# Expert-choice MoE inside a three-layer kernel: one-hot gather and scatter in exact high and low parts, 15 weight slots, weights in 8 KB runs

## Chip, cores and metric

One NeuronCore of a Trainium2 chip runs the whole program in one launch. The metric is device microseconds (us) of that launch. All matrices are float32 in memory; the program may use fp32r (the single-pass float32 form of TensorE) where the values allow it.

## The reference

The program is one block with an expert-choice mixture of experts, followed by two layers of another block. Only the experts of the first block are touched (S = 512 tokens, D = 1024, 16 experts, each takes its 64 best tokens):

```python
def expert_choice_ffn(h, router_w, w_gate, w_up, w_down):
    cap = CAPACITY_FACTOR * T // N_EXPERTS            # 64
    aff = jax.nn.softmax(jnp.einsum('btd,de->bte', h, router_w), axis=-1)
    gate, idx = lax.top_k(jnp.swapaxes(aff, 1, 2), cap)
    xin = jax.vmap(lambda hb, ib: hb[ib])(h, idx)
    hid = jax.nn.silu(jnp.einsum('becd,edf->becf', xin, w_gate)) * jnp.einsum('becd,edf->becf', xin, w_up)
    y = jnp.einsum('becf,efd->becd', hid, w_down) * gate[..., None]
    return scatter_add(y, idx)
...
h2 = modulate(layer_norm(x), sh2, sc2)
x = layer_norm_affine(ALPHA * x + gt2 * expert_choice_ffn(h2, ...), ln2_g, ln2_b)
```

## The kernel before

The tokens stand in NT = 4 tiles `K.x[i]` of 128 tokens by 1024 channels. `first_out` ends the mixer and calls `moe_token` for each token tile: `normed` (L752) writes the normalised tokens `m.h[i]`, PE transposes them (L834), ACT copies them out (L835) and a router product gives the 16 affinities `m.aff`. In `moe`, top-k on VectorE (DVE) turns them into ranks `m.pos`.

The loop over experts goes by pairs (e0, e0 + 1). DVE compares the ranks with a row of numbers: the one-hot matrix P (L895), [token, expert of the pair x slot]. **Gather**: for each of KD = 8 channel blocks, PE multiplies the block of `m.h[i]` by P and sums over the four token tiles (L902); the modulation is applied on the way out of PSUM, on DVE or ACT by turns (L905, L907), which gives XT, [channel, slot]. PE transposes P (L911), ACT copies it to PT (L912), and PE takes each slot's gate value by a product of P with the affinities (L918). **Gate and up**: 64 slots by 1024 outputs in two 64-column tiles of PE, L929. Silu is on ACT (L934), the product with up and the gate value on DVE (L935); PE transposes it (L938), ACT copies it (L946, hidT). **Down** is L952. DVE multiplies by the modulation into Y (L957). **Scatter**: PT times Y, for four token tiles by two halves of 512 channels (L959), and DVE adds the result to x (L967, L969). The last pair scatters into PSUM banks that already hold x (L944, L975) and goes straight to the next LayerNorm (L740, L983).

A product of two float32 operands is one instruction in the program and two records in the trace; fp32r is one record.

Each expert's weights come in twelve loads of 1 MiB, [128, 2, 1024], issued by SP through `K.raw` (L78). The slots are three rings: two of five slots (`K.use_ring(c, 5, 5)`, open from the mixer's end) and `ring2` with eight, opened in `moe`; `turns` says which ring the next load takes. An issue waits on SP's queue until its slot's matmuls are done, and holds what is queued behind it.

PE's order is not the order of the program text: a list scheduler places instructions by readiness and priority, so gathers of the next pair and scatters of the last stand between gate and up matmuls. PSUM has banks for gu (2), tr (2, gather), rt (1), py (1) and sc (2, scatter).

Of the kernel before, what the change touches and what calls it, by code (L numbers as in the profile page):

```python
# [8 lines left out]
F32 = mybir.dt.float32  # L9
# [742 lines left out]

def normed(K, out, x, spread):

    nc = K.nc
    m, r = ln_stats(K, halves(x))
    if spread:
        nc.scalar.activation(out, x, AF.Identity, scale=r, bias=ln_bias(K, m, r))
    else:
        nc.vector.tensor_scalar(out, x, m, r, op0=OP.subtract, op1=OP.mult)  # L760
# [18 lines left out]


def moe_start(K, c):

    nc = K.nc
    m = Moe()
    m.keep = K.pool(c, "e_keep", 1, side="right")
    K.use_ring(c, 5, 5, side="right")
    hp = K.pool(c, "e_h", 1, side="right")
    m.h = [hp.tile([128, D], F32, name=f"h{i}") for i in range(NT)]
    m.aff = m.keep.tile([128, NT, NE], F32, name="aff")
    m.pos = m.keep.tile([128, NT, NE], F32, name="pos")  # L790
    m.cols = m.keep.tile([128, 16], F32, name="ecols")
    m.iota = m.keep.tile([128, CAP], F32, name="iota")
    nc.gpsimd.iota(m.iota, pattern=[[1, CAP]], base=1, channel_multiplier=0, allow_small_or_imprecise_dtypes=True)
    return m


def moe_router(K, m, pool, router_w, mods):
# [7 lines left out]
    m.bias = pool.tile([128, NE], F32, name="bias")  # L805
    rw = pool.tile([128, KD, 128], F32, name="nT")[:, :, :NE]
    nc.sync.dma_start(rw, dram(router_w, 0, [[NE, 128], [128 * NE, KD], [1, NE]]))
    rows = pool.tile([128, 128], F32, name="lt")[:16]
    nc.sync.dma_start(rows, dram(mods, 1024, [[128, 16], [1, 128]]))
    ones = pool.tile([128, 128], F32, name="lt")  # L810
    nc.gpsimd.memset(ones, 1.0)
    p = K.ps("ex")
    nc.tensor.transpose(p[:, :16], rows, K.ident[:16, :16])
    cols = m.cols
    nc.vector.tensor_copy(cols, p[:, :16])
    nc.vector.scalar_tensor_tensor(m.rw[:, :, :NE], rw, -1.0, cols[:, 8:, None].to_broadcast([128, KD, NE]), op0=OP.mult, op1=OP.mult)
# [7 lines left out]
def moe_token(K, m, pool, i):  # L824

    nc = K.nc
    n = m.h[i]
    normed(K, n, K.x[i], i < NT - 1)
    nT = pool.tile([128, KD, 128], F32, name="nT")
    for g in range(2):  # L830
        p = K.ps()
        for j in range(4):
            k = g * 4 + j
            nc.tensor.transpose(p[:, j * 128:(j + 1) * 128], n[:, k * 128:(k + 1) * 128], K.ident)  # L834
        nc.scalar.copy(nT[:, g * 4:g * 4 + 4].rearrange("p a b -> p (a b)"), p)  # L835

    p = K.ps()
# [15 lines left out]
def moe(K, m, wg, wu, wd, mods):  # L853

    nc, tc = K.nc, K.tc
    with ExitStack() as c:
        K.use_banks(c, gu=2, tr=2, rt=1, py=1, sc=2)
        xp = K.pool(c, "e_x", KD)
        gp = K.pool(c, "e_p", 2)

        K.rings.append(K.pool(c, "ring2", 8))
        yp = K.pool(c, "e_y", 1)
        gt2 = K.bcast(yp, mods[3], "gt2")
        turns = itertools.cycle([0, 1] * 5 + [2] * 8)
        with ExitStack() as c2:
# [23 lines left out]
        for e0 in range(0, NE, 2):  # L889

            XT = [xp.tile([128, 2 * CAP], F32, name="XT") for _ in range(KD)]
            P = gp.tile([128, NT, 2, CAP], F32, name="P")
            Pm = P.rearrange("p i e c -> p i (e c)")
            for i in range(NT):
                nc.vector.tensor_tensor(P[:, i], m.iota[:, None, :].to_broadcast([128, 2, CAP]),  # L895
                                        m.pos[:, i, e0:e0 + 2, None].to_broadcast([128, 2, CAP]), op=OP.is_equal)
            for k in range(KD):
                if k % 4 == 0:
                    p4 = K.ps("tr")
                p = p4[:, k % 4 * 128:(k % 4 + 1) * 128]  # L900
                for i in range(NT):
                    nc.tensor.matmul(p, m.h[i][:, k * 128:(k + 1) * 128], Pm[:, i], start=i == 0, stop=i == NT - 1)  # L902
                sh, sc = m.cols[:, k:k + 1], m.cols[:, 8 + k:9 + k]
                if k % 2:
                    nc.scalar.activation(XT[k], p, AF.Identity, scale=sc, bias=sh)  # L905
                else:
                    nc.vector.tensor_scalar(XT[k], p, sc, sh, op0=OP.mult, op1=OP.add)  # L907
            PT = yp.tile([128, S], F32, name="PT")
            pp = K.ps("rt")
            for i in range(NT):  # L910
                nc.tensor.transpose(pp[:, i * 128:(i + 1) * 128], Pm[:, i], K.ident)  # L911
            nc.scalar.copy(PT, pp)  # L912
            y = yp.tile([128, D], F32, name="Y")
            for e in (e0, e0 + 1):
                p = K.ps("rt")
                for i in range(NT):
                    for h in range(2):
                        nc.tensor.matmul(p[h * 64:(h + 1) * 64, 0:1], P[:, i, e - e0], m.aff[:, i, e:e + 1],  # L918
                                         start=i == 0, stop=i == NT - 1, tile_position=(0, h * 64))
# [3 lines left out]
                for w in (wg, wu):  # L923
                    p = K.ps("gu")
                    for k0 in range(0, KD, 2):
                        r = K.raw([128, 2, D], dram(w, (e * D + k0 * 128) * D, [[D, 128], [128 * D, 2], [1, D]]), next(turns))
                        for k in range(k0, k0 + 2):
                            for h in range(2):
                                nc.tensor.matmul(p[h * 64:(h + 1) * 64], XT[k][:, (e - e0) * CAP:(e - e0 + 1) * CAP],  # L929
                                                 r[:, k - k0, h * 512:(h + 1) * 512], start=k == 0, stop=k == KD - 1,  # L930
                                                 tile_position=(0, h * 64))
# [16 lines left out]
                for f0 in range(0, KD, 2):  # L948
                    r = K.raw([128, 2, D], dram(wd, (e * D + f0 * 128) * D, [[D, 128], [128 * D, 2], [1, D]]), next(turns))
                    for f in range(f0, f0 + 2):  # L950
# [907 lines left out]
def first_out(K, F, I, cm, mods):  # L1858

    nc = K.nc  # L1860
    with ExitStack() as c:
# [35 lines left out]
        scan_finish(K, F, 2)  # L1897
        scan_finish(K, F, 3)
        moe_router(K, m, tp, I["router_w"], mods)
        acc.append([K.ps("ex") for _ in range(2)])  # L1900
# [91 lines left out]
```

## Time and profile before

| what | value |
|---|---|
| runs | median 3489.3 us of 3 (3488.88 to 3494.43) |
| profiled execution | 3489.0 us, its span 3487.2 us |
| mean granted clock of TensorE | 0.95 |
| busy over the span | PE 90%, DVE 61%, ACT 39%, POOL (GpSimd) 30% |
| token phase | 760 to 813 us: PE 29.5 us busy, DVE 43.8, ACT 9.8, POOL 8.3 of 53 |
| experts | 813 to 1345 us: PE 519.4 us busy, DVE 99.5, ACT 40.0 of 532; clock 0.98; DMA share 0.92 |
| two layers after them | from 1345 us on |

All times of rows are microseconds from the span's start. A time behind a group of matmuls is from its first start to its modelled end, which overlaps the next; the step from one start to the next is what one costs. `PEclk` is the clock that the throttle granted, 1.00 being 2.4 GHz and 0.50 being 1.2 GHz. The DMA share is the mean busy share of 16 DMA engines; it can read slightly above 1.

### The profile page before, as it was taken

The numbers are of one execution on the slowest core, as the hardware profiler recorded it, in microseconds if no ns is written. First come the engines' busy times: TensorE is split into PE (matmuls) and PEld (weight loads), VectorE is DVE, ScalarE is ACT, GpSimd is POOL, SyncE is SP. The second block draws the span as 40 slices with busy tenths as digits, with TensorE's granted clock in tenths as the row PEclk, the third lists the DMA queues.
The fourth block names the chain that finished last, engine by engine and source line by source line (L and its number), as shares of the span: only waits on it lengthen the run. The fifth ranks groups of instructions, "written<-read, shape, count | busy, mean of one in ns | idle before, by whom it ended". The sixth has DMA issues, their size and how long they took to land. (4 is left out here: it accounts for less than half of the span.)

```text
span 3487.2 us, 52482 instructions
## 1 busy us (share of the span) xinstructions
PE 3130.2 (90%) x20683; PEld 2450.0 (70%) x20683; DVE 2141.1 (61%) x3732; ACT 1356.0 (39%) x2630; POOL 1063.5 (30%) x1071
## 2 busy tenths in 40 slices
PE   6989876777999997999999989998999989989998
PEld 4765455653434334998877678987898977779987
DVE  5667984463211116765767666757856776858657
ACT  3446564221000003443456543434433455634433
POOL 3134473040000004342431243424432341233423
PEclk9999987988999998999999999999999999999999
DMA  5335265548999992322332123222322322213222
GB/s 208 112 118 192 99 200 169 198 151 323 400 387 373 376 352 79 111 84 98 104 96 66 39 71 109 85 97 95 100 97 97 98 79 64 67 49 111 84 99 95
DMA packets 284775, 508.53 MB, mean 146 GB/s; under 512 B 30430, under 2 KB 206384, under 8 KB 279408
## 3 DMA queue, kind: packets, MB, share of 16 engines
q1 hardware_dynamic: 267520, 487.35, 39.7%
q10 hardware_dynamic: 16336, 17.13, 1.5%
q8 instruction: 162, 2.65, 0.3%
q0 software_dynamic: 672, 0.70, 0.1%
q14 instruction: 85, 0.70, 0.1%
HBM read 473.66 MB, written 31.47 MB: 145 GB/s over the span
## 5 line engine op out<-in xcount | busy, mean ns | idle before, releaser
L100 DVE TENSOR_TENSOR wl<-raw,wh 128x1024 fp32r<-128x1024 f32 (+2 forms) x346 | 395.0, 1155 | 213.3 <-ACT wh L99 212.7
L105 PE MATMUL ps<-hTh,wh 128*128 128x256 f32 (+1 forms) x1656 | 493.4, 301 | 14.7 <-ACT hTh L238 12.5
L99 ACT CAST wh<-raw 128x1024 fp32r<-128x1024 f32 (+2 forms) x348 | 312.6, 920 | 458.0 <-PE ps L107 163.2
L106 PE MATMUL ps<-hTl,wh 128*128 128x256 f32 (+1 forms) x1656 | 489.2, 297 | 0.5 <-DVE hTl L239 0.5
L107 PE MATMUL ps<-hTh,wl 128*128 128x256 f32 (+1 forms) x1656 | 476.8, 297 | 3.4 <-DVE wl L100 3.3
L105 PEld LDWEIGHTS ps<-hTh,wh 128*128 128x128 f32 x1656 | 320.8, 195 | 27.9 <-ACT hTh L238 14.2
L297 POOL TENSOR_TENSOR tmp<-raw 128x512 f32<-128x512 f32 x176 | 246.4, 1407 | 292.0 <-DMA raw<-in_w_ffn_gate_dram 231.4
L106 PEld LDWEIGHTS ps<-hTl,wh 128*128 128x128 f32 x1656 | 321.2, 194 | 10.3 <-DVE hTl L239 1.7
L106 PE MATMUL ps<-wl,hh 128*128 128x512 f32 x832 | 324.0, 389 | 0.0
L107 PEld LDWEIGHTS ps<-hTh,wl 128*128 128x128 f32 x1656 | 314.5, 194 | 12.6 <-DVE wl L100 5.4
L107 PE MATMUL ps<-wh,hl 128*128 128x512 f32 x832 | 322.4, 389 | 0.0
L105 PE MATMUL ps<-wh,hh 128*128 128x512 f32 x832 | 303.6, 390 | 2.8 <-DVE hl L511 2.8
L115 POOL TENSOR_TENSOR rs_o<-rs_t,mhalf 128x1 f32<-128x1 f32 (+1 forms) x46 | 36.1, 811 | 848.7 <-DVE rs_t L114 847.7
L100 DVE TENSOR_TENSOR wl<-tmp,wh 128x1024 fp32r<-128x1024 f32 x176 | 244.6, 1390 | 56.9 <-ACT wh L99 55.8
L297 POOL TENSOR_TENSOR tmp<-raw,tmp 128x512 f32<-128x512 f32 x88 | 122.6, 1393 | 480.0 <-DVE wl L100 480.0
L929 PE MATMUL gu<-raw,XT 128*64 128x512 f32 x1024 | 250.7, 600 | 0.0
L99 ACT CAST wh<-tmp 128x1024 fp32r<-128x1024 f32 x176 | 184.4, 1048 | 92.8 <-POOL tmp L297 63.7
L105 PEld LDWEIGHTS ps<-wh,hh 128*128 128x128 f32 x832 | 155.5, 188 | 34.1 <-DVE hl L511 3.3
L107 PEld LDWEIGHTS ps<-wh,hl 128*128 128x128 f32 x832 | 156.2, 188 | 32.5
L106 PEld LDWEIGHTS ps<-wl,hh 128*128 128x128 f32 x832 | 156.3, 188 | 31.7
L929 PEld LDWEIGHTS gu<-raw,XT 128*64 128x64 f32 x1024 | 70.4, 136 | 133.7 <-issue 125.7
L294 DVE TENSOR_TENSOR u<-u,ps 128x256 f32<-128x256 f32 x308 | 127.6, 414 | 50.6 <-PE ps L107 27.2
(558 smaller groups left out, 7381.6 us busy)
## 6 DMA issues: line engine op xcount, KB each, us to landing
raw<-in_exp_w_gate_dram SPq DMA_DIRECT2D x64, 1024.0 KB
raw<-in_exp_w_up_dram SPq DMA_DIRECT2D x64, 1024.0 KB
raw<-in_exp_w_down_dram SPq DMA_DIRECT2D x64, 1024.0 KB
raw<-in_w_ffn_gate_dram SPq DMA_DIRECT2D x44, 1024.0 KB
raw<-in_w_ffn_up_dram SPq DMA_DIRECT2D x44, 1024.0 KB
raw<-in_w_ffn_down_dram SPq DMA_DIRECT2D x44, 1024.0 KB
raw<-in_w_ada_dram SPq DMA_DIRECT2D x24, 1024.0 KB
raw<-in_w_in_dram SPq DMA_DIRECT2D x36, 512.0 KB
```

Source lines behind the costliest of these rows:

```text
L99: nc.scalar.copy(h3, src)
L100: (engine or nc.vector).tensor_tensor(l3, src, h3.bitcast(F32), op=OP.subtract)
L105: mm(out, lhs[0], rhs[0], start=start, stop=False)
L106: mm(out, lhs[0], rhs[1], start=False, stop=False)
L107: mm(out, lhs[1], rhs[0], start=False, stop=stop)
L115: self.pow = nc.gpsimd.tensor_tensor(o[:, :n], t[:, :n], self.mhalf[:, :n], op=OP.pow)
L294: self.K.nc.vector.tensor_tensor(o, a, b, op=OP.add)
L297: self.K.nc.gpsimd.tensor_tensor(o, a, b, op=op)
L929: nc.tensor.matmul(p[h * 64:(h + 1) * 64], XT[k][:, (e - e0) * CAP:(e - e0 + 1) * CAP], r[:, k - k0, h * 512:(h + 1) * 512], start=k == 0, ...
```

## The change

Four things, all in the experts:

- **Gather.** Each normalised token is split into `hh` (the value as fp32r, an ACT copy) and `hl` (the rest, a POOL subtract), in halves of 512 channels (L856 and L857 of the changed file). P is written as fp32r, for four experts at once, so the gather runs once per two pairs with 256 columns and two fp32r products (`hh`, `hl`) per token tile. The gather's tiles take half a PSUM bank each.
- **Scatter.** Y is split likewise into Yh and Yl (DVE product, ACT copy, DVE subtract); PT is fp32r, and each scatter tile is two fp32r products.
- **Slots.** `ring2` has five slots instead of eight, 15 in all; `turns` follows.
- **Loads.** A load takes two neighbouring rows per partition, so that each partition reads 8 KB in one run. Channel 2p + r of a block of 256 then stands on partition p, and everything that meets the weights' rows follows that order: `normed` writes it, the router weights and modulation columns are loaded in it, and silu and the product are written through `pairs_apart` (the product in two halves of 256 columns).

```diff
+def pairs_apart(x):
+    n = x.shape[1] // 256
+    return x.rearrange("p (a r q) -> p a q r", a=n, r=2)
+def in_pairs(x):
+    return x.rearrange("p (a q r) -> p a q r", a=x.shape[1] // 256, r=2)
...
-def normed(K, out, x, spread):
+def normed(K, out, x, m, r, nm=None):
+    out, x = pairs_apart(out), in_pairs(x)
...
-    m.h = [hp.tile([128, D], F32, name=f"h{i}") for i in range(NT)]
+    m.hh, m.hl = ([hp.tile([128, D], F32R, name=f"{n}{i}") for i in range(NT)] for n in ("mh", "ml"))
...
+    for h, l, x in zip(halves(m.hh[i]), halves(m.hl[i]), n):
+        nc.scalar.copy(h, x)
+        nc.gpsimd.tensor_tensor(l, x, h.bitcast(F32), op=OP.subtract)
...
-        gp = K.pool(c, "e_p", 2)
-        K.rings.append(K.pool(c, "ring2", 8))
+        gp = K.pool(c, "e_p", 1)
+        K.rings.append(K.pool(c, "ring2", 5))
-        turns = itertools.cycle([0, 1] * 5 + [2] * 8)
+        turns = itertools.cycle([0, 1] * 5 + [2] * 5)
...
+            if e0 % 4 == 0:
+                XT = [xp.tile([128, 4 * CAP], F32, name="XT") for _ in range(KD)]
+                P = gp.tile([128, NT, 4, CAP], F32R, name="P")
...
-                    nc.tensor.matmul(p, m.h[i][:, k * 128:(k + 1) * 128], Pm[:, i], start=i == 0, stop=i == NT - 1)
+                    for i in range(NT):
+                        for n, h in enumerate((m.hh[i], m.hl[i])):
+                            nc.tensor.matmul(p, h[:, k * 128:(k + 1) * 128], Pm[:, i], start=i + n == 0, stop=i + n == NT)
...
-                        r = K.raw([128, 2, D], dram(w, (e * D + k0 * 128) * D, [[D, 128], [128 * D, 2], [1, D]]), next(turns))
+                        r = K.raw([128, 2, D], dram(w, (e * D + k0 * 128) * D, [[2 * D, 128], [D, 2], [1, D]]), next(turns))
...
-                nc.scalar.activation(sl, pg[0], AF.Silu)
-                nc.vector.scalar_tensor_tensor(sl, sl, gc, pg[1], op0=OP.mult, op1=OP.mult)
+                nc.scalar.activation(pairs_apart(sl), in_pairs(pg[0]), AF.Silu)
+                for a in range(2):
+                    q = slice(a * 256, a * 256 + 256)
+                    nc.vector.scalar_tensor_tensor(pairs_apart(sl[:, q]), pairs_apart(sl[:, q]), gc, in_pairs(pg[1][:, q]),
+                                                   op0=OP.mult, op1=OP.mult)
...
-                    nc.vector.tensor_tensor(y[ro, sl], py[h * 64:(h + 1) * 64], gt2[ro, sl], op=OP.mult)
+                    y = tp.tile([128, 512], F32, name="sil")[ro]
+                    nc.vector.tensor_tensor(y, py[h * 64:(h + 1) * 64], gt2[ro, sl], op=OP.mult)
+                    nc.scalar.copy(yh[ro, sl], y)
+                    nc.vector.tensor_tensor(yl[ro, sl], y, yh[ro, sl].bitcast(F32), op=OP.subtract)
...
-                nc.tensor.matmul(p, PT[:, i * 128:(i + 1) * 128], y[:, h * 512:(h + 1) * 512], start=start, stop=True)
+                for n, t in enumerate((yh, yl)):
+                    nc.tensor.matmul(p, PT[:, i * 128:(i + 1) * 128], t[:, h * 512:(h + 1) * 512], start=start and n == 0, stop=n == 1)
...
```

The scheduler's order changes with it. First PE around the transposes of silu (L938 before, L966 after; gu are gate and up, tr the gather, sc the scatter, py the down product), at an expert in the middle of the loop. Before:

```order
L929 MATMUL gu<-raw,XT 64x512 x4
L902 MATMUL tr<-P,h_7403 128x128
L902 MATMUL tr<-P,h_7404 128x128
L902 MATMUL tr<-P,h_7405 128x128
L902 MATMUL tr<-P,h_7406 128x128
L938 MATMUL rt<-ident,sil 128x128 x4
L902 MATMUL tr<-P,h_7403 128x128
L902 MATMUL tr<-P,h_7404 128x128
L902 MATMUL tr<-P,h_7405 128x128
L902 MATMUL tr<-P,h_7406 128x128
L952 MATMUL py<-raw,hidT 64x512 x12
```

And now, at two experts that follow one another:

```order
L943 MATMUL rt<-aff,P 64x1 x8
L954 MATMUL gu<-raw,XT 64x512 x12
L966 MATMUL rt<-ident,sil 128x128 x4
L980 MATMUL py<-raw,hidT 64x512 x4
L943 MATMUL rt<-aff,P 64x1 x8
L980 MATMUL py<-raw,hidT 64x512 x12
L954 MATMUL gu<-raw,XT 64x512 x32
L966 MATMUL rt<-ident,sil 128x128 x4
L980 MATMUL py<-raw,hidT 64x512 x4
```

Before, gather products stood on either side of the transposes; now gate and up, transposes and down follow one another with nothing between. Over the stage the runs of gather products between others go from 42 to 18, those of scatter products from 42 to 32.

Second, POOL in the token phase (rs_o is the reciprocal root of a LayerNorm; raw the weights of the mixer's last product). Before:

```order
L115 TENSOR_TENSOR rs_o<-rs_t,mhalf 128x8 x2
L1877 TENSOR_TENSOR raw<-raw 128x1024 x4
L811 MEMSET lt 128x128
L1877 TENSOR_TENSOR raw<-raw 128x1024 x4
L115 TENSOR_TENSOR rs_o<-rs_t,mhalf 128x1 x11
```

And now (L1910 is L1877 of before):

```order
L115 TENSOR_TENSOR rs_o<-rs_t,mhalf 128x8
L1910 TENSOR_TENSOR raw<-raw 128x1024 x4
L115 TENSOR_TENSOR rs_o<-rs_t,mhalf 128x8
L1910 TENSOR_TENSOR raw<-raw 128x1024 x4
L115 TENSOR_TENSOR rs_o<-rs_t,mhalf 128x1 x3
L857 TENSOR_TENSOR ml_7407<-fin,mh_7403 128x512 x2
L115 TENSOR_TENSOR rs_o<-rs_t,mhalf 128x1 x2
L857 TENSOR_TENSOR ml_7408<-fin,mh_7404 128x512 x2
L115 TENSOR_TENSOR rs_o<-rs_t,mhalf 128x1 x2
L857 TENSOR_TENSOR ml_7409<-fin,mh_7405 128x512
L115 TENSOR_TENSOR rs_o<-rs_t,mhalf 128x1
```

The subtracts for `hl` stand between the reciprocals of the token tiles, and one reciprocal of the mixer moved behind four multiplies of raw.

## Rows read from the trace of the kernel before

**Rows 1.** The page, busy time by engine.

```profile
PE 3130.2 (90%) x20683; PEld 2450.0 (70%) x20683; DVE 2141.1 (61%) x3732; ACT 1356.0 (39%) x2630; POOL 1063.5 (30%) x1071
```

**Rows 2.** Stretches: busy by engine (instructions), then PEclk, DMA share, GB/s.

```profile
813.00:1345.00 532.00, 519.35 (x2544) 213.07 (x2544) 99.45 (x198) 40.04 (x74) 1.05 (x2) 0.98 0.92 359
850.00:900.00 50.00, 50.00 (x242) 20.41 (x240) 10.22 (x20) 3.01 (x6) 0.00 (x0) 1.00 1.02 409
```

**Rows 3.** Waits of SP's queue, 813 to 1320: total us, times, longest.

```profile
SPq L78 <- PE gu L929: 295.2, 118, 18.4
SPq L78 <- PE py L952: 109.8, 51, 9.5
```

**Rows 4.** Timeline of SP's queue (start, us with waiting): first refill, last weight loads.

```profile
824.61 0.37 SPq L78 DMA_DIRECT2D raw<-in_exp_w_down_dram  x1
...
1285.31 11.71 SPq L78 DMA_DIRECT2D raw<-in_exp_w_down_dram  x4
```

**Rows 5.** Timeline of PE (start, us, records) at two places of the stage.

```profile
900.81 1.98 PE L959 MATMUL sc<-Y,PT 128*128 128x512 f32 x4
902.73 1.94 PE L929 MATMUL gu<-raw,XT 128*64 128x512 f32 x8
904.59 1.16 PE L902 MATMUL tr<-P,h 128*128 128x128 f32 x8
905.68 0.63 PE L918 MATMUL rt<-aff,P 128*64 128x1 f32 x16
...
1131.07 1.95 PE L902 MATMUL tr<-P,h 128*128 128x128 f32 x16
1132.86 0.60 PE L911 MATMUL rt<-ident,P 128*128 128x128 f32 x4
```

**Rows 6.** Timeline of PE outside it: fp32r products of 512 and 256 columns.

```profile
754.72 0.39 PE L107 MATMUL ps<-wh,fin 128*128 128x512 f32 x1
...
756.99 0.39 PE L105 MATMUL ps<-wh,fin 128*128 128x512 f32 x1
...
1399.78 0.28 PE L107 MATMUL ps<-T2h,wl 128*128 128x256 f32 x1
...
1402.78 0.28 PE L105 MATMUL ps<-T4h,wh 128*128 128x256 f32 x1
```

**Rows 7.** Waits of PE, 813 to 1337: total us, times, longest.

```profile
PE rt L938 <- DVE sil L935: 4.2, 4, 1.2
PE py L952 <- ACT hidT L946: 3.7, 5, 0.7
...
PE rt L918 <- ACT PT L912: 1.5, 2, 0.7
```

**Rows 8.** Groups by line, 813 to 1346: busy us, mean ns, idle before.

```profile
L969 DVE TENSOR_TENSOR x<-x,sc 128x512 f32<-128x512 f32 x48 | 33.0, 687 | 87.8 <-PE sc L959 87.8
...
L935 DVE SCALAR_TENSOR_TENSOR sil<-sil,gc,gu 128x512 f32<-128x512 f32 x16 | 11.9, 746 | 44.1 <-PE gu L929 28.7 <-issue 15.0
...
L946 ACT COPY hidT<-rt 128x512 f32<-128x512 f32 x16 | 9.4, 585 | 74.3 <-PE rt L938 74.3
```

**Rows 9.** Stretches behind three of PE's waits (columns as in rows 2).

```profile
1101.60:1108.40 6.80, 5.96 (x16) 2.18 (x18) 0.00 (x0) 0.58 (x1) 0.00 (x0) 0.50 0.08 20
...
1169.90:1176.70 6.80, 6.07 (x16) 2.00 (x18) 0.00 (x0) 0.58 (x1) 0.00 (x0) 0.50 0.19 69
1234.00:1242.00 8.00, 6.36 (x46) 2.52 (x44) 0.90 (x2) 0.59 (x1) 0.00 (x0) 1.00 1.00 376
```

**Rows 10.** Timeline of DVE at the stage's end.

```profile
1341.33 0.70 DVE L740 BATCH_NORM_STATS2 bn<-sc 128x6 f32<-128x512 f32 x1 [1.87 <-PE sc L959]
```

**Rows 11.** Timelines of POOL and of DVE at the mixer's end.

```profile
710.49 10.64 POOL L1877 TENSOR_TENSOR raw<-raw 128x1024 f32<-128x1024 f32 x4
...
713.30 2.84 DVE L1656 TENSOR_TENSOR x<-x,fin 128x512 f32<-128x512 f32 x1
```

**Rows 12.** A stretch with loads of the modulation weights (columns as in rows 2).

```profile
20.00:30.00 10.00, 5.71 (x30) 2.20 (x33) 8.66 (x17) 0.00 (x0) 4.57 (x7) 1.00 1.02 416
```

More of the change, by code (lines that the diff above doesn't have):

```diff
@@ L750, in ln_rows @@
     K.nc.vector.tensor_scalar(out, x, m, r, op0=OP.subtract, op1=OP.mult)
[L753 removed]
+def normed(K, out, x, m, r, nm=None):
     nc = K.nc
[L756 to L758 removed]
+    out, x = pairs_apart(out), in_pairs(x)
+    if nm is not None:
+        nc.scalar.activation(out, x, AF.Identity, scale=r, bias=nm)
     else:
@@ L805, in moe_router @@
     m.bias = pool.tile([128, NE], F32, name="bias")
[L806 to L809, printed above, removed]
+    nT = pool.tile([128, KD, 128], F32, name="nT")
+    rw = nT[:, 0].rearrange("p (a x) -> p a x", a=KD // 2)
+    nc.sync.dma_start(rw, dram(router_w, 0, [[2 * NE, 128], [256 * NE, KD // 2], [1, 2 * NE]]))
+    rows = nT[:8, 1:3].rearrange("p a b -> p (a b)")
+    rw = rw.rearrange("p a (r e) -> p (a r) e", r=2)
+    nc.sync.dma_start(rows, dram(mods, 1024, [[256, 8], [1, 256]]))
     ones = pool.tile([128, 128], F32, name="lt")
@@ L812, in moe_router @@
     p = K.ps("ex")
-    nc.tensor.transpose(p[:, :16], rows, K.ident[:16, :16])
+    for r in range(2):
+        nc.tensor.transpose(p[:, r * 8:r * 8 + 8], rows[:, r::2], K.ident[:8, :8])
     cols = m.cols
-    nc.vector.tensor_copy(cols, p[:, :16])
+    nc.vector.tensor_copy(cols.rearrange("p (v r) -> p v r", r=2), p[:, :16].rearrange("p (r v) -> p v r", r=2))
     nc.vector.scalar_tensor_tensor(m.rw[:, :, :NE], rw, -1.0, cols[:, 8:, None].to_broadcast([128, KD, NE]), op0=OP.mult, op1=OP.mult)
@@ L826, in moe_token @@
     nc = K.nc
-    n = m.h[i]
-    normed(K, n, K.x[i], i < NT - 1)
+    n = m.n
+    mean, r = ln_stats(K, halves(K.x[i]))
+    nm = ln_bias(K, mean, r) if i < NT - 1 else None
+    for o, x in zip(n, halves(K.x[i])):
+        normed(K, o, x, mean, r, nm)
     nT = pool.tile([128, KD, 128], F32, name="nT")
@@ L908, in moe @@
-            PT = yp.tile([128, S], F32, name="PT")
+            if e0 % 4 == 0:
+                XT = [xp.tile([128, 4 * CAP], F32, name="XT") for _ in range(KD)]
+                P = gp.tile([128, NT, 4, CAP], F32R, name="P")
+                Pm = P.rearrange("p i e c -> p i (e c)")
+                for i in range(NT):
+                    nc.vector.tensor_tensor(P[:, i], m.iota[:, None, :].to_broadcast([128, 4, CAP]),
+                                            m.pos[:, i, e0:e0 + 4, None].to_broadcast([128, 4, CAP]), op=OP.is_equal)
+                for k in range(KD):
+                    if k % 2 == 0:
+                        p4 = K.ps("tr")
+                    p = p4[:, k % 2 * 256:(k % 2 + 1) * 256]
+                    for i in range(NT):
+                        for n, h in enumerate((m.hh[i], m.hl[i])):
+                            nc.tensor.matmul(p, h[:, k * 128:(k + 1) * 128], Pm[:, i], start=i + n == 0, stop=i + n == NT)
+                    sh, sc = m.cols[:, k:k + 1], m.cols[:, 8 + k:9 + k]
+                    if k % 2:
+                        nc.scalar.activation(XT[k], p, AF.Identity, scale=sc, bias=sh)
+                    else:
+                        nc.vector.tensor_scalar(XT[k], p, sc, sh, op0=OP.mult, op1=OP.add)
@@ L948, in moe @@
                 for f0 in range(0, KD, 2):
-                    r = K.raw([128, 2, D], dram(wd, (e * D + f0 * 128) * D, [[D, 128], [128 * D, 2], [1, D]]), next(turns))
+                    r = K.raw([128, 2, D], dram(wd, (e * D + f0 * 128) * D, [[2 * D, 128], [D, 2], [1, D]]), next(turns))
                     for f in range(f0, f0 + 2):
@@ L1898, in first_out @@
         scan_finish(K, F, 3)
+        m.n = [F.fin.tile([128, 512], F32, name="fin") for _ in range(2)]
         moe_router(K, m, tp, I["router_w"], mods)
```

28 lines of the change are left out of this document (7 added, 21 removed).

## Prediction, before the changed kernel ran

> **What bounds the kernel now.** I first read the page's line of engines: TensorE (PE) is busy 90% of the span, no other engine above 61% [rows 1]. But the change touches one stage only, the experts, so I read that stage by itself, in the view of stretches: from 813 to 1345 us PE is busy 519 of 532 us, and in 850 to 900 all 50 of 50, while the DMA engines are at share 1.02 with 409 GB/s there and 0.92 over the stage [rows 2]. Both look full, so the question is which ends last. The waits of SP's queue, which issues the weight loads, answer it: it waits 295 us for gate and up matmuls (L929) and 110 us for down matmuls (L952) to free a slot [rows 3], and the four last are issued from 1285.3 over 11.71 us, so by 1297 us [rows 4], 48 us before the stage ends. DMA waits for PE; PE is the bound, DMA is close behind. So what the change takes off PE counts in full until the loads are reached.
>
> **Gather.** Before: 8 pairs x 8 channel blocks x 4 token tiles x 2 records, which is 512 records of 128x128. Sixteen in a row start 1.79 us before the next instruction, 0.112 us each [rows 5]. Where a run of eight stands between 64-column gate/up matmuls it takes 1.09 us instead of 0.90, so about 0.2 us per run goes into changing over. The order of before has 42 runs: 512 x 0.112 + 42 x 0.2 = 65.7 us. After: 4 groups x 8 blocks x 4 tiles x 2 (high, low) = 256 fp32r records of 128x256, in 18 runs. Such records start 0.12 us apart in the feed-forward stage: 25 steps in 3.00 us [rows 6]. So 256 x 0.12 + 18 x 0.2 = 34.3, **-31 us**. With no cost of changing over it would be -27.
>
> **Scatter.** 64 tiles of 128x512, each two records before. Four records next to gate/up take 1.92 us [rows 5], less 0.2 that is 0.43 each. After, a tile is two fp32r records (Yh, Yl), which start 0.227 us apart: 10 steps in 2.27 us [rows 6]. The last 8 tiles, at the stage's end, are paced by VectorE (below), so 56 tiles count: before 112 x 0.43 + 42 runs x 0.2 = 56.6; after 112 x 0.227 + 32 runs x 0.2 = 31.8. **-25 us** (-23 without the runs).
>
> **What shrinks comes out of the cover.** Each expert has a chain PE gate/up, ACT silu, DVE product, PE transposes, ACT copy, PE down product. PE hides it by other matmuls where the order has some to put there. It waited 4 times for the product (4.2 us, at most 1.2) and 5 times for the copy (3.7 us) [rows 7]; three of these are doubles, both waits of one expert, at 1101, 1169 and 1236. With half as many gather records and whole pairs without any, the scheduler's new order has 10 places where gate/up, transposes and down stand directly behind one another, 2 more with the second wait alone and 1 with the first. At 4.2/4 = 1.05 and 3.7/5 = 0.74 us, and 0.1 more since the product is now two halves of 256 columns (the 512 took 0.746 [rows 8], two halves lie between that and twice that): 11 x 1.15 + 12 x 0.74 = 21.5 against 7.9, **+14 us**. For a silu that writes with a stride there is no row; between an ACT pass over 512 columns, 0.585 [rows 8], and twice that I take the first, since it handles as many elements.
>
> **The clock.** Behind the double of 1101, PE ran at a granted clock of 0.50, the lower of its two levels (1.2 GHz), for 6.8 us, and likewise behind the one of 1169; behind the one of 1236 it stayed at 1.00 [rows 9]. The first two had a wait for the copy of PT just ahead of the chain as well (L918, twice in all, 0.7 us each [rows 7]), the third only gate/up matmuls. Each fall costs 6.8/2 = 3.4 us, and before has two. Of the ten new doubles one is like the first, nine like 1236. I take three falls, **+3 us**; bounds are none (-7) and all ten (10 x 3.4 - 6.8 = +27).
>
> **DVE beside PE.** A tile's two records now take 0.45 us, but DVE's x += tile takes 0.687 [rows 8] with two PSUM banks to run ahead in. Between gate/up matmuls that is covered. The first scatter has six tiles together: **+2** (0 to 2). At the end DVE's statistics take 0.70 us per tile [rows 10], eight in sequence, so the faster last scatter gives nothing; and Y passes ACT (a copy of 512 columns, 0.585) and a DVE subtract (priced as the add, 0.687 [rows 8]) before it, **+1**.
>
> **Token phase (760 to 813).** DVE is nearly continuous, POOL only does small reciprocals. The change puts eight POOL subtracts 128x512 there (L857), with reciprocals that DVE waits for queued behind some of them, eight ACT casts (ACT has the room), and four `normed` halves more. How DVE does beside such POOL work the trace shows at 710 to 720: while POOL multiplies tiles, 2.66 us each, L1656, an add of 512 columns, takes 2.84 us [rows 11]; one of as many columns, an operand of it in PSUM and POOL idle, takes 0.687 [rows 8]. From below nothing (POOL falls into DVE's gaps), from above eight times half of 2.66 (half the columns), or 11. I take **+2**: nearer the low end, because each subtract falls where DVE waits for that token's logits anyhow. The Trainium skill says more plainly why ("SBUF — State Buffer", section "Who interferes with whom"): VectorE and GpSimd share a port pair that is locked exclusively. By that rule the sum would carry the 11 in place of the 2; the 2.84 us agrees with it, the position of the subtracts decides.
>
> **Weight loads.** 192 loads of 1 MiB; 15 slots instead of 18 means 177 come after the first slot is freed, about 11 us into the stage (the first such issue is at 824.61 [rows 4], the stage starts at 813). Runs of 8 KB (the modulation weights at the start) moved 416 GB/s [rows 12], against 409 with 4 KB: 2.52 us per load. So 11 + 177 x 2.52 = 457 us after the stage's start the last load has landed, and with some 14 us behind it (its matmuls, Y, the last scatter and statistics) the loads allow a stage of 471 us, or 478 with 2.56 us. PE will need 532 - 34 = 498. The loads stay hidden, and the 8 KB order by itself gives **0**; if the cover goes, it is worth 177 x 0.04 = 7 us. Three slots fewer cost 0 so long as the lead of 15 holds: gate, up and down of a pair take PE 24 x 1.72 = 41 us (eight records a load, 1.86 less the changing over [rows 5]), their 24 loads 60, so a pair without a gather eats some four slots of lead and the pair with gather and scatter gives them back.
>
> **Sum:** -31 - 25 + 14 + 3 + 2 + 1 + 2 = -34 us. Against the profiled execution's own 3489.0 (span 3487.2) that is 3455; the median of the runs is 3489.3, the same within 0.3.
>
> **The rivals.**
> (A) The chain stays covered: no more waits and falls than before. Then -56 + 3 + 2 = -51 or so, and there the loads (471 to 478) come in sight: **3438**. Against it: the order shows ten bare chains.
> (B) The clock falls behind every double and POOL's subtracts block DVE: -56 + 14 + 27 + 3 + 11 = -1, **3488**. For it: two falls of three doubles before. Against: the one at 1236, which most of the new ones resemble, kept its clock.
> (C) Slower: the loads become the bound with 15 slots. Place: SP's queue at L78, PE then waiting for raw. It decides from the price at which 11 + 177 t + 14 exceeds 532, t = 2.86 us or 367 GB/s; below that rate every load adds. For it: DMA share 0.92 over the stage [rows 2] and three slots fewer. Against it: 409 and 416 GB/s [rows 2, 12], the former held for 50 us on end. At 360 GB/s t is 2.91 and the stage 540: **3498**. The Trainium skill ("DMA: Bandwidth & Descriptors", section "Where 436 GB/s comes from") would have it so: between HBM and SBUF it lets about 358 GB/s per core bind, which by an estimate makes 2.93 us per load, a stage of 543 us and 3500. By that rule slower; the trace, with 409 GB/s, disagrees on this run with one core, so it gets a small chance.
> (D) The change doesn't do what it says on PE: a 128x256 fp32r record of the gather takes twice 0.12, say because high and low weights alternate. Then the gather gives nothing and the sum is -3: **3486**. Against it: the feed-forward rows have the same shape, with a new weight load each time [rows 6].
>
> **How the numbers follow.** A measurement of this kernel tells apart about 0.2%, 7 us. Forecast (3444 to 3470): 0.72. A 0.12, B 0.09, C 0.05, D 0.02. The predicted time is the forecast's, **3455 us**. The range reaches down to A with the loads' floor, 3434, and up through most of what lies between forecast and B (all ten falls of the clock but no blocking gives 3479): **3434 to 3479**. Faster by over 0.2%: forecast, A and half of B, 0.88; same: the other half of B and D, 0.07; slower: C, 0.05.
>
> **What would show it.** In the profile after: PE's stage about 34 us shorter; gather x256 and scatter records 0.12 and 0.23 us apart; waits of PE for sil and hidT near 12 and 9 us; about three stretches of 6 to 7 us at clock 0.5; SP still waiting for PE at L78, and PE waiting for raw under 5 us; the token phase at 53 us or up to 2 more; nothing different beyond 1345 but the shift. I am wrong if PE waits for raw for tens of us (C), if the clock row shows many dips (B), or if the gather's records start 0.24 us apart (D).

## The result, and the profile after

Changed kernel: median 3439.98 us (3437.62 to 3444.53, 4 runs); before, beside it, 3489.09 (3485.37 to 3494.43). Ratio 0.9861, interval 0.9849 to 0.9874: faster by 1.4%. The profiled execution has 3439.81 us and a span of 3438.0, so 49.2 us less than the span before. The forecast was 34 us less.

The page's engines and the stretches answer to [rows 1, 2]; the stage now goes from 810 to 1292:

```profile
PE 3064.7 (89%) x20428; PEld 2418.2 (70%) x20428; DVE 2160.7 (63%) x3749; ACT 1384.5 (40%) x2657; POOL 1072.7 (31%) x1079
```

```profile
810.00:1292.00 482.00, 455.24 (x2288) 182.40 (x2288) 119.18 (x215) 62.91 (x92) 2.15 (x3) 0.99 0.97 397
850.00:900.00 50.00, 45.87 (x214) 16.74 (x212) 13.03 (x22) 6.37 (x9) 0.00 (x0) 0.93 1.01 419
...
892.00:898.80 6.80, 6.12 (x15) 1.71 (x16) 0.00 (x0) 0.58 (x1) 0.00 (x0) 0.51 1.01 414
```

PE is no longer full (455 of 482 us), and the loads run at 419 GB/s almost without a pause: DMA share 0.97 over the stage, 0.92 before. The waits of PE from 810 to 1292 (total, times, longest), against [rows 7], and those of SP's queue, against [rows 3]:

```profile
PE rt L966 <- DVE sil L962: 10.5, 12, 1.1
PE py L980 <- ACT hidT L974: 8.1, 12, 0.7
PE py L1008 <- DVE sil L986: 1.5, 1, 1.5
```

```profile
SPq L78 <- PE gu L954: 176.6, 89, 28.7
SPq L78 <- PE py L980: 98.9, 50, 8.1
SPq L78 <- DMA raw<-in_exp_w_gate_dram: 44.4, 25, 2.1
```

SP still waits for PE most, but now also for loads on their way (110 us over the three weights), which it did not before. PE does not yet wait for a load worth a line.

Where the time went. I call stage the way from the first gather product to the end of DVE's last statistics, and take both ends from the timelines. Before it went from 813.6 to 1345.8, by these two rows:

```profile
813.63 1.19 PE L902 MATMUL tr<-P,h 128*128 128x128 f32 x4 [0.73 <-DVE P L895]
...
1345.06 0.69 DVE L740 BATCH_NORM_STATS2 bn<-py 128x6 f32<-128x512 f32 x1
```

After, it goes from 810.0 to 1291.7:

```profile
810.04 0.55 PE L926 MATMUL tr<-P,mh 128*128 128x256 f32 x1 [0.94 <-DVE P L918]
```

```profile
1290.98 0.68 DVE L740 BATCH_NORM_STATS2 bn<-py 128x6 f32<-128x512 f32 x1
```

So the stage went from 532.1 to 481.6 us, **-50.5**; what lies ahead of it -3.6, behind it +4.9. Of the last two I put only +0.2 us down to the change (the token phase, below): over all the runs of this document the part ahead varies from 808 to 818 us and the part behind from 2141 to 2149, in nearly the same code. Part of that is the clock: the half-clock stretches ahead of the mixer's end sum to 122.9 us before and 112.6 here (and to 116 to 130 in the runs below), those behind the stage to 149.9 and 156.4. The rest is not explained.

PE inside the stage, each record priced by the step from its start to the next start, so that a wait is charged to the record ahead of it:

| | before | after | difference |
|---|---|---|---|
| gather | 68.3 us, 512 records | 36.0, 256 | -32.3 |
| scatter | 63.2 | 39.8 | -23.4 |
| gate and up | 243.9 | 240.3 | -3.6 |
| transposes of silu | 13.9 | 21.5 | +7.6 |
| down, gate values, transposes of P, x | 141.1 | 139.8 | -1.3 |

In gate and up the new waits for silu hide a larger gain: without the waits behind them, gate and up fell from 242.1 to 230.6 us, and the transposes of silu rose from 10.1 to 13.4.

The new records cost what the old trace said. PE's timeline, start and duration: gather 0.12 us apart; a scatter tile 0.23 + 0.24 us, four records between two gate/up groups 1.12 us against 1.92 [rows 5].

```profile
823.75 0.28 PE L926 MATMUL tr<-P,ml 128*128 128x256 f32 x1
823.87 0.28 PE L926 MATMUL tr<-P,mh 128*128 128x256 f32 x1
...
1226.91 0.50 PE L992 MATMUL sc<-Yh,PT 128*128 128x512 f32 x1
1227.24 0.39 PE L992 MATMUL sc<-Yl,PT 128*128 128x512 f32 x1
1227.47 0.40 PE L992 MATMUL sc<-Yh,PT 128*128 128x512 f32 x1
1227.71 0.39 PE L992 MATMUL sc<-Yl,PT 128*128 128x512 f32 x1
1228.03 0.65 PE L954 MATMUL gu<-raw,XT 128*64 128x512 f32 x2
```

A bare chain, as it stands ten times in the order:

```profile
1240.27 5.37 PE L954 MATMUL gu<-raw,XT 128*64 128x512 f32 x24
1246.46 0.92 PE L966 MATMUL rt<-ident,sil 128*128 128x128 f32 x4 [0.82 <-DVE sil L962]
1248.06 1.94 PE L980 MATMUL py<-raw,hidT 128*64 128x512 f32 x8 [0.67 <-ACT hidT L974]
```

### The profile page after: what moved, and what is told of

It is laid out like the page before. It is cut to its first block, busy times and chain, and to the rows that moved or that the text cites. A ratio compares the mean times of both kernels' runs of the same rounds, so it can differ in the third digit from the quotient of the medians.

```text
span 3438.0 us, 52002 instructions
## 1 busy us (share of the span) xinstructions
PE 3064.7 (89%) x20428; PEld 2418.2 (70%) x20428; DVE 2160.7 (63%) x3749; ACT 1384.5 (40%) x2657; POOL 1072.7 (31%) x1079
## 5 line engine op out<-in xcount | busy, mean ns | idle before, releaser
L100 DVE TENSOR_TENSOR wl<-tmp,wh 128x1024 fp32r<-128x1024 f32 x176 | 247.6, 1407 | 56.6 <-ACT wh L99 55.5
L954 PE MATMUL gu<-raw,XT 128*64 128x512 f32 x1024 | 235.9, 597 | 0.3 <-ACT sil L959 0.3
```

Source lines behind the costliest of these rows:

```text
L100: (engine or nc.vector).tensor_tensor(l3, src, h3.bitcast(F32), op=OP.subtract)
L954: nc.tensor.matmul(p[h * 64:(h + 1) * 64], XT[k][:, e % 4 * CAP:(e % 4 + 1) * CAP], r[:, k - k0, h * 512:(h + 1) * 512], start=k == 0, sto ...
```

## The experiments

"Reserve" is the time from the last weight load's last packet to PE's first product with it, both from the trace: 9.8 us in the changed kernel, 33.5 in e7_8kb_alone, which has the work of before; it is not given where the loads come in 4 KB runs. Ratios are against the kernel before in the same session, whose median there was 3488.6 to 3491.5 us. The stage is read from one trace of each kernel; those of before, e5 and e7, which have the same work on PE, lie within 2.1 us.

| kernel | median us | ratio, interval | stage us | reserve us |
|---|---|---|---|---|
| before | 3489.1 | | 532.1 | |
| changed | 3440.0 | 0.9861 (0.9849 to 0.9874) | 481.6 | 9.8 |
| e1_plain_product | 3441.6 | 0.9858 (0.9840 to 0.9875) | 479.0 | 6.6 |
| e2_4kb | 3445.9 | 0.9879 (0.9865 to 0.9894) | 485.5 | |
| e3_gather_only | 3466.7 | 0.9937 (0.9920 to 0.9955) | 506.1 | 22.8 |
| e4_scatter_only | 3464.9 | 0.9928 (0.9913 to 0.9943) | 506.2 | 25.3 |
| e5_before_15 | 3489.1 | 0.9997 (0.9987 to 1.0006) | 530.2 | |
| e6_cover | 3435.5 | 0.9840 (0.9824 to 0.9857) | 473.4 | 1.4 |
| e7_8kb_alone | 3484.7 | 0.9976 (0.9967 to 0.9986) | 530.0 | 33.5 |
| e8_12slots | 3450.9 | 0.9881 (0.9866 to 0.9896) | 486.5 | 6.7 |
| e9_late_split | 3433.0 | 0.9839 (0.9824 to 0.9855) | 473.1 | 1.3 |
| e10_cover_4kb | 3450.1 | 0.9886 (0.9869 to 0.9902) | 485.2 | |
| e11_late_casts | 3434.1 | 0.9834 (0.9820 to 0.9847) | 473.3 | 1.4 |

Theory: the gain is PE's own time, and PE stays the bound. Rival: the loads have become the bound, so that gains count in part, and the 8 KB runs are part of them.

**The two halves of the gain.**

> The changed kernel with the scatter as before (PT and Y in float32, one product per tile); split gather for four experts, 15 slots and 8 KB runs stay. Theory (the gain is PE's own time): PE's stage gets the scatter's 23 us back, less 3 bare chains fewer in the order at 2 us each: 477 + 23 - 6 = 494 us, time about 3457. Rival (the loads set the end already, so that what PE saves counts only in part): less than 12 us above the changed kernel, 3452 or less.

```diff
-            PT = yp.tile([128, S], F32R, name="PT")
+            PT = yp.tile([128, S], F32, name="PT")
...
-                for n, t in enumerate((yh, yl)):
-                    nc.tensor.matmul(p, PT[...], t[...], start=start and n == 0, stop=n == 1)
+                nc.tensor.matmul(p, PT[...], y[...], start=start, stop=True)
...
```

> The changed kernel with the gather as before (tokens and one-hot matrix in float32, two experts at a time, no split of the tokens); split scatter, 15 slots and 8 KB runs stay. Theory (PE's own time): PE's stage gets the gather's 32 us back, less 4 bare chains fewer at 2 us each, and some changing over more: 477 + 32 - 8 + 3 = 504 us, time about 3467; the token phase without POOL's subtracts 0 to 1 us shorter. With e3_gather_only the two parts add up to the whole within 5 us. Rival (the loads set the end): 3452 or less. Second rival (the split of the tokens costs the token phase several us): the token phase here 3 us or more shorter than in the changed kernel.

```diff
-    m.hh, m.hl = (... F32R ...)
+    m.h = [hp.tile([128, D], F32, name=f"h{i}") for i in range(NT)]
...
-                        for n, h in enumerate((m.hh[i], m.hl[i])):
-                            nc.tensor.matmul(p, h[...], Pm[:, i], ...)
+                    nc.tensor.matmul(p, m.h[i][...], Pm[:, i], start=i == 0, stop=i == NT - 1)
...
```

Without the split scatter the stage is 24.5 us longer (scatter 62.8 us on PE, 37.1 for the gather), without the split gather 24.6 longer (gather 68.3, scatter 38.0). The gather alone is worth 26.0 us and the scatter alone 25.9 of the stage, 51.9 together against 50.5 at once: they add up, so the rival falls for the kernel as it is. e4 came out as expected (3465 for 3467). e3 did not: the theory had a stage 17 us longer and about 3457 us, and 24.5 and 3466.7 came out. The scatter's 23 us came back, but the three chains fewer gave only 2.9 us of waits (18.6 to 15.7) and not 6, PE waited 3.1 us for Y, and half-clock stretches behind chains took 13.6 us instead of 10.2. In e4 the transposes of silu cost 15.1 us instead of 21.5: of the gather's 32 us, some 6 are lost in bare chains. The second rival of e4 holds: from the mixer's last split on POOL to the first one-hot matrix it takes 111.6 us, with the split tokens 115.0, before 114.8.

**The chain, and the loads' order.**

> The changed kernel, but silu and its product are written in plain order (one product of 512 columns instead of two strided halves) and PE's transposes read every second column instead. Theory (PE is the bound, and the two halves overlap with the first transposes): the chain gets shorter by some 0.1 us per bare expert, 13 of them, so the stage of PE 1 to 2 us shorter than 477.3 us, time 3438 to 3440. Rival (the strided instructions themselves are what the chain pays: silu 1.09 against 0.60 us, product 1.30 against 0.75): 13 x 0.55 = 7 us shorter, 3433. A third case, slower by over 5 us, would mean that transposes with a column stride cost PE extra.

```diff
-                nc.scalar.activation(pairs_apart(sl), in_pairs(pg[0]), AF.Silu)
-                for a in range(2):
-                    ...
+                nc.scalar.activation(sl, pg[0], AF.Silu)
+                nc.vector.scalar_tensor_tensor(sl, sl, gc, pg[1], op0=OP.mult, op1=OP.mult)
...
-                    nc.tensor.transpose(ph[...], sl[:, q * 128:(q + 1) * 128], K.ident)
+                    nc.tensor.transpose(ph[...], sl[:, q // 2 * 256 + q % 2:q // 2 * 256 + 256:2], K.ident)
```

The same chain as that of 1240.27 above, in e1:

```profile
1251.63 0.74 PE L963 MATMUL rt<-ident,sil 128*128 128x128 f32 x4 [0.91 <-DVE sil L960]
```

The stage is 2.6 us shorter, PE's waits for the product are 10.6 us against 10.5. The two halves (0.65 us each) take 0.09 us off the wait of a bare chain, 0.82 against 0.91, since the first two transposes start behind the first half; but the third waits for the second half, and the four take 0.92 us instead of 0.74. Silu itself takes 1.09 us with its stride and 0.60 without, but PE has its up products meanwhile. In the runs' times 2.6 us does not show.

> The same kernel as e1_plain_product, but weights, tokens and modulation columns in plain channel order and the loads in 4 KB runs as in the kernel before; 15 slots and the split gather and scatter stay. Theory (the loads run without a pause in the changed kernel and end 10 us before PE needs the last one): a load at 2.56 instead of 2.505 us puts the last landing some 10 us later, PE's cover is used up, PE waits for raw by 0 to 5 us, time 0 to 5 us above e1_plain_product. Rival 1 (the loads are hidden as I predicted, the 8 KB order is worth nothing): same as e1_plain_product within 1 us and 5 us or more of slack left. Rival 2 (the loads are already the bound and the 8 KB order is where part of the gain came from): 10 us or more above e1_plain_product.

```diff
-    return x.rearrange("p (a r q) -> p a q r", a=n, r=2)
+    return x
...
-  ... [[2 * D, 128], [D, 2], [1, D]]
+  ... [[D, 128], [128 * D, 2], [1, D]]
...
```

PE's waits from 812 to 1298, and a stretch of the loads:

```profile
PE rt L960 <- DVE sil L957: 10.6, 11, 1.2
PE py L974 <- ACT hidT L968: 8.1, 12, 0.7
PE gu L951 <- DMA raw<-in_exp_w_up_dram: 4.6, 8, 0.6
PE gu L951 <- DMA raw<-in_exp_w_gate_dram: 4.2, 6, 1.6
```

```profile
900.00:1000.00 100.00, 96.54 (x502) 42.16 (x500) 25.05 (x44) 11.94 (x20) 0.00 (x0) 1.00 1.02 409
```

409 GB/s instead of 419, and 8.8 us of PE waiting for weights that e1 does not have. The stage is 6.5 us longer, between theory (0 to 5) and its second rival (10): the 8 KB runs are worth about 6 us of the stage here. That is a net figure: behind its chains e2 had 3.4 us at half clock and e1 10.2, which took some 3 us off the difference.

**The parts that were to cost or bring nothing.**

> The kernel before with ring2 of five slots instead of eight, nothing else. Theory (before, PE is the bound with some 40 us between a load's landing and its use): three slots fewer take 7.5 us of that lead, PE still waits for no load, time as before within 4 us (3485 to 3493). Rival (the slots' loss is a cost that the other parts of the change had to pay back): 7 us or more slower than before, with PE waiting for raw.

```diff
-        K.rings.append(K.pool(c, "ring2", 8))
+        K.rings.append(K.pool(c, "ring2", 5))
...
-        turns = itertools.cycle([0, 1] * 5 + [2] * 8)
+        turns = itertools.cycle([0, 1] * 5 + [2] * 5)
```

The same time, as theory has it, and PE waits for no load: the kernel before does not need slots 16 to 18.

> The kernel before (float32 gather and scatter, two experts at a time, 18 slots) with the channel order and the 8 KB runs of the change alone. Theory (the loads are hidden in the kernel before): the rate rises from about 409 to 419 GB/s where the loads run without a pause, SP waits that much longer for PE, time as before within 4 us (3485 to 3493); silu's strided writes cost 1 or 2 us of that at most. Rival (the loads' rate already counts before): 6 us or more faster, 3483 or less.

```diff
-                        r = K.raw([128, 2, D], dram(w, ..., [[D, 128], [128 * D, 2], [1, D]]), next(turns))
+                        r = K.raw([128, 2, D], dram(w, ..., [[2 * D, 128], [D, 2], [1, D]]), next(turns))
...
```

The channel order of the change goes with it, in `normed`, the router weights and the columns too, so the edit reaches into the token phase. The median, 3484.7, is just outside the expected span on the fast side, and 6.9 us below that of before in its session (3491.5). But the stage gained 2.1 us only, 1.7 of that by half a clock fall less, with 33.5 us of reserve: not the loads. 3.2 us come from the token phase, 111.6 us on the way named above against 114.8: in the new order the router's bias product stands earlier on PE, 34.6 us behind the start of POOL's last split instead of 39.1. That this is the cause is not shown. The rest of the 6.9 is not separated from the spread outside the stage. So the 8 KB runs bring nothing to the loads' end before, and 6 us once the rest is faster.

> The changed kernel with ring2 of two slots, 12 in all instead of 15. Its order has 7 bare chains instead of 10. Theory (slots count by what they hold when the stage begins, since the loads run without a pause afterwards): three loads more, 7.5 us, must come after the first slot is freed, so the last landing moves from 460 to 467 us after the stage's start, PE's reserve of 9 us goes to about 2, less what the covered chains take: PE waits for raw by 0 to 6 us, time 3438 to 3446. Rival (12 slots are too few to bridge a pair without a gather, whose loads take some 20 us longer than its matmuls): PE waits for raw by 10 us or more in the pairs without a gather and the time is over 3450.

```diff
-        K.rings.append(K.pool(c, "ring2", 5))
+        K.rings.append(K.pool(c, "ring2", 2))
...
-        turns = itertools.cycle([0, 1] * 5 + [2] * 5)
+        turns = itertools.cycle([0, 1] * 5 + [2] * 2)
```

Slower by 11 us, outside theory's span and in the rival's (over 3450), but not for the rival's reason: PE has no line of waiting for raw. The loads did what theory said: the last one landed 467.6 us after the stage's start, against 459.6 with 15 slots. But PE got slower by itself. The order changed with the slots: scatter runs fell from 31 to 16, longer ones in which PE waits for DVE's x (3.0 us, 12 times; scatter 47.2 us against 39.8), and 17.0 us at half clock against 10.2. So three slots cost the loads 8 us here, and what that alone would cost the time stays open.

**Is PE's loss in the chain worth what it seems, and where do the loads stop it?**

> The kernel of e1_plain_product with the experts' program order turned: after the gate and up matmuls of an expert come the first load's matmuls of the next expert's gate, then this expert's transposes of silu, the next load's matmuls, then this expert's down product (not at every fourth expert, where the gather is in between). All else is the same. In the order 3 bare chains are left of 10. Theory (PE is the bound now, with the bare chains as its loss and the loads 7 to 10 us behind): PE's waits for sil and hidT fall from 10.6 + 8.1 us to 5 or less, the falls of the clock go, which would be worth 14 + 5 = 19 us, but the loads catch up after 7 to 10 us: PE then waits for raw, the stage of PE is 465 to 470 us, time 3430 to 3434. Rival 1 (the loads are no floor there): the whole 19 us, PE's stage 457, time 3421. Rival 2 (the loads set the end already in the changed kernel): nothing gained, 3438 to 3443.

```diff
+                    if pend and w is wg and k0 == 0:
+                        with K.behind(mm):
+                            ph = turned(pend[0])
+                    if pend and w is wg and k0 == 2:
+                        with K.behind(mm):
+                            down(e - 1, ph)
```

Here `turned` is the transposes of the expert before, `down` its down product, and mm the last product of the load just used. PE's waits from 812 to 1286 and its timeline late in the stage:

```profile
PE gu L996 <- DMA raw<-in_exp_w_up_dram: 4.1, 7, 0.7
PE py L935 <- ACT hidT L929: 3.4, 5, 0.7
PE gu L996 <- DMA raw<-in_exp_w_gate_dram: 3.0, 6, 0.6
PE py L935 <- DMA raw<-in_exp_w_down_dram: 1.6, 3, 0.6
...
PE rt L924 <- DVE sil L1012: 1.2, 2, 0.9
```

```profile
1194.71 1.94 PE L996 MATMUL gu<-raw,XT 128*64 128x512 f32 x8 [0.55 <-DMA raw<-in_exp_w_up_dram]
1197.20 1.94 PE L996 MATMUL gu<-raw,XT 128*64 128x512 f32 x8 [0.55 <-DMA raw<-in_exp_w_up_dram]
1199.70 1.94 PE L996 MATMUL gu<-raw,XT 128*64 128x512 f32 x8 [0.56 <-DMA raw<-in_exp_w_up_dram]
```

The waits for sil and hidT fell from 18.7 to 4.6 us and no half-clock stretch is left behind a chain. In their place stand 8.7 us of waiting for loads: late in the stage PE takes a load every 2.49 us, the price of one load, and not the 1.72 of its products. PE's stage, up to the start of its last scatter record, is 469.1 us, as theory had it (465 to 470), and 5.6 us below e1, not the 19 of rival 1; the median, 3435.5, is 1.5 above theory's span. (Without their waits gate and up rose by 4.7 us, 230.0 to 234.7, which no run explains.) So in the changed kernel PE is the bound with the loads 10 us behind; in e6 both are.

> The kernel of e6_cover with weights, tokens and modulation columns in plain channel order and loads in 4 KB runs. Theory (in e6_cover the loads set the end, 177 of them after the first free slot): each takes 2.56 instead of 2.505 us, the last lands 9 to 10 us later and the stage ends that much later, time 8 to 11 us above e6_cover, about 3445, with PE waiting for raw. Rival (PE's own work still sets most of the end there): 0 to 4 us above e6_cover.

The edit is that of e2 on e6. The stage is 11.8 us longer (485.2), with 18.9 us of waits for loads: where the loads set the end, the 8 KB runs count in full. By 419 and 409 GB/s a load of 1 MiB takes 2.50 and 2.56 us, and 177 x 0.06 is 11 us; the 0.055 of the expectation was a little low. The median is 14.6 us above e6_cover's, more than the 8 to 11 expected: 2.3 us of that is the plain order's token phase (117.4 us on the way named above against 115.0).

**The token phase.**

> The kernel of e6_cover with POOL's eight subtracts of the token split issued in one piece behind the last token's reciprocals, beside top-k, instead of between the tokens; each token keeps its own buffers for the normalised halves. ACT's casts stay where they are. In the runs so far the way from the mixer's last split on POOL to the first one-hot matrix takes 115.0 us with the split of the tokens and 111.6 without it. Theory (the subtracts beside the tokens' DVE work are what costs the 3.4): 111.6 to 112.5 us, the stage as in e6_cover, time 3 us below it, 3431 to 3434. Rival 1 (ACT's casts in the token chain cost it): still 114.5 to 115, time as e6_cover. Rival 2 (the subtracts slow top-k instead, since DVE and POOL work on SBUF together there): the tokens end 3 us earlier and top-k takes that much longer, no gain.

```diff
-        nc.gpsimd.tensor_tensor(l, x, h.bitcast(F32), op=OP.subtract)
...
+        with K.behind(K.pow):
+            for i in range(NT):
+                for h, l, x in zip(halves(m.hh[i]), halves(m.hl[i]), m.n[i]):
+                    nc.gpsimd.tensor_tensor(l, x, h.bitcast(F32), op=OP.subtract)
```

Nothing gained: 115.2 us. I took that for rival 1, ACT's casts, and moved them as well:

> The kernel of e9_late_split with ACT's eight casts of the token split also moved behind the last token (behind its last exponential), so that ACT has nothing between a token's normalised halves and the copies of its transposes. Theory, taken up after e9_late_split (the casts, 1.1 us per token in front of those copies, are what the token split costs): the way from the mixer's last split to the first one-hot matrix falls from 115.2 to 111.6 to 112.5 us, the stage stays at 473 us as the loads set its end, time 3 us below e6_cover and e9_late_split, 3429 to 3433 us. Rival (the loads' first free slot does not move with the stage's start, so the gain is lost in PE's waits for raw): 112 us on that way, but a stage 3 us longer and the same time.

```diff
-        nc.scalar.copy(h, x)
...
+        with K.behind(K.pow, m.last):
+                    nc.scalar.copy(h, x)
```

111.8 us, the whole 3.4. But the two traces side by side say that it was not the casts. In e9 the first three tokens' LayerNorms are as early as in e11 though the casts stand there. The loss comes with the fourth, where POOL's subtracts already run (they start right behind the last reciprocal). Counted from POOL's last split, e9 is 0.25 us behind e11 when DVE starts to normalise that token, and 2.1 when it has done so; two scalings of affinities (1.11 and 0.70 us in e9, 0.23 each in e11) add most of the rest, and at the first step of top-k it is 3.4. The groups of DVE from 760 to 800, e9 first, then e11, where the subtracts wait for the late casts and so start behind the last token:

```profile
L760 DVE TENSOR_SCALAR fin<-x,mv,rs_o 128x512 f32<-128x512 f32 x2 | 3.2, 1686 | 0.7 <-POOL rs_o L115 0.7
...
L871 DVE TENSOR_SCALAR aff<-aff,est 128x16 f32<-128x16 f32 x4 | 2.3, 566 | 0.1
```

```profile
L760 DVE TENSOR_SCALAR fin<-x,mv,rs_o 128x512 f32<-128x512 f32 x2 | 1.4, 798 | 0.7 <-POOL rs_o L115 0.7
...
L869 DVE TENSOR_SCALAR aff<-aff,est 128x16 f32<-128x16 f32 x4 | 0.9, 216 | 0.1
```

So the first theory, POOL beside the tokens' DVE work, stands, and e9 had not fully removed it; a run with late casts and early subtracts, which would prove it, is not there. The 3 us do not show in the medians (3435.5, 3433.0, 3434.1, whose runs spread over 6 to 8 us); they are read from the trace alone. e6, e9 and e11 all beat the changed kernel by 4 to 7 us in the median, and the stage by 8; the intervals of the ratios of e6 and e9 still overlap that of the changed kernel.

## Why the prediction was right, and where its size was off

The measured 3440 lies in the range (3434 to 3479) and on the side given 0.88. What bounds the stage, the gather's gain, the bare chains and the loads' floor were right; the saving was 49 us in the span instead of 34. Of the cases the time is nearer to rival A (3438) than to the forecast (3455), but that is luck: A wanted the chain to stay covered, and all ten bare chains stood there and cost what was forecast. Step by step:

- **Gather, -31: right.** Measured -32.3, by the steps of PE.
- **Scatter, -25: too large.** All 64 tiles gave -23.4, but 3.5 of that is the last eight, which the sum left out. The 56 that it counts went from 55.8 to 35.9 us, -19.9, not from 56.6 to 31.8.
- **The chain, +14: right in sum, its parts otherwise.** 10 bare chains as read from the order, and 12 waits for each operand (11 and 12 in the prediction). PE waited 0.88 and 0.68 us each time, not 1.15 and 0.74: 18.6 us against 7.9, +10.7. The 1.05 was a mean of two kinds in the trace of before, 1.20 us in the two chains with a wait for PT just ahead and 0.91 in the other two, and the halves of the product shorten the wait by 0.09 (e1). What they cost stands in the transposes instead, +3.3 us, of which e1 gets 1.9 back. Together +14.0.
- **The clock, +3: wrong in sign.** Two falls in ten bare chains, 6.8 and 3.4 us long, which cost 5.1 us against 6.8: -1.7. The first of them is the chain with a wait for PT ahead of it, as argued; over all runs the argument holds (last section).
- **DVE beside the first scatter, +2: about right.** Its six tiles stand together from 884.49 us on, twelve records with starts 0.36 us apart instead of 0.23: some 1.5 us, inside the scatter's 35.9. **Tail, +1:** the way from the start of PE's last scatter record to the end of the statistics grew from 1.6 to 4.3 us, since PE, but not DVE, got faster there; with the 3.5 us that PE gained on those eight tiles this comes to -0.8. Leaving these tiles out of the sum was right.
- **Token phase, +2: right by two errors.** +0.2 came out, of +3.4 for the split tokens and -3.2 for the router's order, which I had not priced. That is luck as well.
- **What was not in the sum: gate and up, -11.5.** The sum put them at nothing; without the waits behind them they fell from 242.1 to 230.6 us. The steps between 64- and 128-column products went from 192 to 142, and the mean step inside gate and up from 0.210 to 0.206 us. The sum priced this change only behind a run of gather or scatter. There is a price ahead of one too: the last gate or up record there takes 0.52 us instead of 0.42, 70 times before and 42 now, 2.8 us. The rest stays open: gate and up and the number of changes go together over the runs (134 and 230.0 us in e1, 190 and 241.9 in e7), but no run separates them.
- **8 KB runs and slots, 0: half wrong.** I forecast 498 us of PE against 471 for the loads, with 7 us of worth "if the cover goes". PE came to 482, the reserve to 9.8 us, and there the 8 KB order is worth 6 (e2 against e1). The 15 slots alone cost nothing before (e5). The floor itself was right: the last load was to land 457 us after the stage's start and did at 459.6, and where the loads set the end, in e6, the stage is 473.
- **Rival C and the Trainium skill's 358 GB/s** ("DMA: Bandwidth & Descriptors", section "Where 436 GB/s comes from"): the loads ran at 419 GB/s from 850 to 1250 us with this one core working; the trace disagrees with the rule as a limit here.

So the mechanism was right and the size off. Gather, scatter, chain, gate and up, and the tail make -32.3 - 19.9 + 14.0 - 11.5 - 0.8 = -50.5, the stage's difference, with the clock's -1.7 inside these steps. The terms that were mis-sized are gate and up (nothing booked, a gain of 11.5 us found), the clock (+3 booked, -1.7 found) and, the other way, the scatter (its gain booked 5 us too high).

## What to carry to other kernels

When the bound engine and the next one are 20 us apart, price the second as a floor with the same care as the gain: here 19 us of PE's waits and clock falls, once covered, were worth 6, mostly because the loads took over, and the load format, worth nothing before, was then worth 12. Read the scheduler's new order for the places where a chain lost its cover, and price each by the wait in the trace, and where an operation is cut in two, price both the earlier start of what follows and its later end. Compare runs by a stretch with fixed ends: 3 us of gain or loss could be read in the traces and in no median.

## What the runs showed of the hardware that was not expected

- 8 KB runs per partition moved 419 GB/s for 400 us on end (the changed kernel, 850 to 1250 us), 4 KB runs 409 (e2, the same stretch): 2.50 and 2.56 us per MiB.
- A half-clock stretch followed 2 of 10 bare chains in the changed kernel; two of three before. Over the kernels of the table, PE waited for both operands of a chain 60 times. Ten times a wait of PE for the copy of PT stood just ahead, and 9 of these went with a fall to half clock; without it 11 of 50 did, 8 of them in e4 and e8.
- DVE's normalising of 128x512 in SBUF took 1.69 us beside POOL's subtracts and 0.80 without; top-k's maxima took 0.68 us each in both (e11, beside the subtracts from 796 to 806 us and behind them). The Trainium skill ("SBUF — State Buffer", section "Who interferes with whom") speaks of an exclusive lock; the first row agrees. The second does not speak against it, since that section of the Trainium skill exempts instructions with at most one SBUF input outside the two-port modes.
- Nearly the same code ahead of the mixer's end came to POOL's last split at 694 to 702 us in the profiles, with 113 to 130 us of it at half clock.
